# Two value stages of an expert layer: ScalarE's copy, cast and small copy of each block, marked to stand block by block

## The chip, the core and the metric

The kernel runs on one core of one Trainium2 chip. The metric is the device time of one execution in microseconds (us); the time before is the median of three runs, 1945.05 us (1939.61 to 1948.28). The core has five engines that work side by side, each through its own queue in order: TensorE (PE, matrix multiplications into PSUM), VectorE (DVE), ScalarE (ACT), GpSimd (POOL) and SyncE (SP, which here only issues loads). An engine whose next instruction waits for a semaphore stands still, and all that is queued behind that instruction stands with it. Transfers from memory run on 16 DMA engines beside them.

## What is computed

A decoder layer: modulation from a condition vector, a mixing part (sparse attention and retention), and a feed-forward part that picks, for each of 256 tokens and 8 heads, 16 of 16384 experts of one neuron each. The change concerns the end of the feed-forward part:

```
def peer_ffn(h, w_q, sub_keys, w_u, w_v):
    ...
    experts = jnp.take_along_axis(cand_i, pick, axis=-1)
    gates = jax.nn.softmax(top_s, axis=-1)
    ...
    def chunk(args):
        hc, ec, gc = args
        a = jnp.einsum('cd,ced->ce', hc, w_u[ec]).astype(F32)
        coef = (gc * jax.nn.gelu(a)).astype(dt)
        return jnp.einsum('ce,ced->cd', coef, w_v[ec])
```

## The kernel before, in words

For 192 of the tokens the kernel doesn't gather experts: it runs over all 16384 in 128 blocks of 128 experts, first the rows of `w_u` (u stages), then those of `w_v` (value stages), with a coefficient that is zero where a token didn't pick the expert. It does so in two halves of 64 blocks: u stage 1, value stage 1, u stage 2, value stage 2. The other 64 tokens are served by gathers of rows (`gather`, line 800, an indirect DMA on POOL's queue), each followed by one step on DVE over 128x2048 numbers (line 841 or 847). Those steps are spread over the stages by the tables `STEPS`; value stage 1 has 44 of them in its first 58 blocks.

A value stage is the loop of `v_group`. For block j of a stage:

- ScalarE copies the 128x192 coefficients X of the block, rounded to float32r, into a tile `cc` (line 936; here "copy of activations"). There are three buffers of `cc`, so the copy for block j waits until TensorE is through with block j-3.
- DVE subtracts to get the part lost by rounding (line 937), into the same `cc` tile; ScalarE then copies 64 columns of that to their place between the two (line 938; "small copy"). It waits for line 937 of the same block.
- SP loads 1 MB of `w_v` into a `raw` tile (line 147; five buffers). ScalarE rounds it into `whi` (line 156, "cast of the chunk", three buffers), DVE subtracts to get the rest, `wlo` (line 157, two buffers).
- TensorE does 20 multiplications with 512 columns (line 960): 8 that need `whi` and the `cc` tile, 8 that need `wlo`, 4 that need `whi` and the small copy. They add up in eight PSUM banks over all 64 blocks.

The program isn't executed in the order of the source. A scheduler orders the instructions of each engine by its own estimate of time, except those that are marked by `tc.keep_in_program_order` (called `pin` here): among themselves these stay in the order in which they are written. Before, the loads on SP, the gathers on POOL and the steps of lines 841 and 847 on DVE are marked; ScalarE's and DVE's part of a block are not. Lines 156 and 157 lie in the helper `split_to`, and line 147 in `load`.

## Time and profile before

| what | value |
|---|---|
| median of three runs | 1945.05 us |
| the profiled execution: its time, and its span from first to last instruction | 1943.4 us, 1941.6 us |
| busy: TensorE, VectorE, ScalarE, GpSimd | 1826.8, 1479.4, 699.4, 348.6 us |
| mean granted TensorE clock | 0.972 of full speed |
| u stage 1 ends, value stage 1 runs | 1002.6, 1002.6 to 1324.2 us |
| u stage 2 | 1324.2 to 1616.5 us |
| value stage 2 | 1616.5 to 1911.8 us |

The stages before 1002.6 us (the mixing part, the choice of experts and u stage 1) and after are untouched. The engines work at the same time, so their busy times don't add up to the span. Where one of them waits for another counts only if it lies on the chain that ends last.

### The profile page before, as it was taken

To read this page: it belongs to the slowest core of one execution; us is meant where nothing else is said; L and a number is where in the kernel's file an instruction comes from. 1 tells how busy PE (TensorE), PEld (TensorE's weight loads), DVE (VectorE), ACT (ScalarE), POOL (GpSimd) and SP (SyncE) were. 2 spreads that over 40 slices of the span, in tenths; PEclk is the share of its full clock that TensorE was granted. 3 is DMA by queue.
4 is the path that set the end of the run, shared out by engine and by line. 5 is a ranking of instruction groups with operands and counts; after the bars stand their busy time and mean duration, and the time that the engine had idled before them with its cause. 6 is when DMAs were issued, how large, how long until landed. Compare 5 with 4: busy or idle time off the path is not lost.

```text
span 1941.6 us, 28423 instructions
## 1 busy us (share of the span) xinstructions
PE 1826.8 (94%) x11302; PEld 1594.3 (82%) x11302; DVE 1479.4 (76%) x2247; ACT 699.4 (36%) x1192; POOL 348.6 (18%) x254
## 2 busy tenths in 40 slices
PE   5899899999987999989999999999999999999995
PEld 4798778788766899989997767779999998777773
DVE  7877888889985898487578888874455557899875
ACT  3444353635434421021134444451111114555552
POOL 1000001011010012102123323221111212344210
PEclk9999998989988999999999999999999999999998
DMA  8989888989993589989989999989999989999981
GB/s 341 381 310 358 324 303 271 346 287 377 374 321 134 185 297 386 424 319 376 361 357 402 348 382 372 340 307 375 397 357 360 361 303 376 383 394 383 388 323 44
DMA packets 94312, 651.86 MB, mean 336 GB/s; under 512 B 11410, under 2 KB 11586, under 8 KB 18402
## 3 DMA queue, kind: packets, MB, share of 16 engines
q1 hardware_dynamic: 66818, 467.78, 63.6%
q0 software_dynamic: 27360, 182.26, 24.2%
q8 instruction: 89, 1.46, 0.3%
q14 instruction: 45, 0.36, 0.0%
HBM read 643.92 MB, written 4.21 MB: 334 GB/s over the span
## 4 chain that ended last, share of the span: by engine, by line
PE 73%; DVE 11%; DMA 6%; issue 6%; ACT 3%; POOL 0%; SPq 0%; ACTq 0%; POOLq 0%; DVEq 0%
PE acc L960 30%; PE psU L1058 27%; PE psN L449 4%; DVE wlo L157 3%; DMA raw<-in_adaT 2%; DVE raw L197 2%; PE psA L235 2%; PE psD L350 2%; ACT whi L156 2%; PE pg L1043 1%; DMA raw<-in_winA 1%; PE psA L236 1%; PE bkB L350 1%; DMA x2d<-xT 1%; PE bkC L350 1%
## 5 line engine op out<-in xcount | busy, mean ns | idle before, releaser
L157 DVE TENSOR_TENSOR wlo<-raw,whi 128x2048 fp32r<-128x2048 f32 (+2 forms) x215 | 479.3, 2239 | 139.3 <-ACT whi L156 90.0
L1058 PE MATMUL psU<-xT,raw 128*128 128x160 f32 x4096 | 570.8, 301 | 5.8 <-ACT ge L1063 4.5
L1058 PEld LDWEIGHTS psU<-xT,raw 128*128 128x128 f32 x4096 | 560.2, 191 | 6.5 <-ACT ge L1063 4.6
L156 ACT CAST whi<-raw 128x2048 fp32r<-128x2048 f32 (+2 forms) x215 | 400.7, 1869 | 228.0 <-PE psA L235 40.7
L960 PE MATMUL acc<-whi,cc 128*128 128x512 f32 x1512 | 376.3, 396 | 16.7 <-ACT whi L156 16.7
L960 PEld LDWEIGHTS acc<-whi,cc 128*128 128x128 f32 x1512 | 286.6, 190 | 89.4 <-ACT whi L156 19.8
L960 PE MATMUL acc<-wlo,cc 128*128 128x512 f32 x1008 | 257.1, 395 | 2.3 <-DVE wlo L157 2.3
L197 DVE SCALAR_TENSOR_TENSOR raw<-raw,crow 128x2048 f32<-128x2048 f32 x96 | 219.3, 2286 | 21.5 <-DMA raw<-in_adaT 21.4
L960 PEld LDWEIGHTS acc<-wlo,cc 128*128 128x128 f32 x1008 | 164.6, 164 | 66.9 <-DVE wlo L157 5.1
L449 PE MATMUL psN<-whi,act 128*128 128x512 f32 x512 | 166.1, 400 | 2.3 <-ACT sg L628 2.3
L1064 DVE TENSOR_TENSOR X<-X,ge 128x160 f32<-128x160 f32 (+19 forms) x94 | 26.0, 278 | 156.2 <-ACT ge L1063 146.6
L1060 ACT ACTIVATE X<-psU 128x160 f32<-128x160 f32 (+19 forms) x102 | 25.6, 252 | 330.8 <-PE psU L1058 330.7
L449 PEld LDWEIGHTS psN<-whi,act 128*128 128x128 f32 x512 | 95.9, 188 | 25.0 <-ACT sg L628 2.7
L936 ACT CAST cc<-X 128x192 fp32r<-128x192 f32 x128 | 44.8, 353 | 197.1 <-PE acc L960 197.1
L449 PE MATMUL psN<-wlo,act 128*128 128x512 f32 x256 | 103.3, 404 | 3.0 <-DVE wlo L157 2.9
L235 PE MATMUL psA<-act,whi 128*128 128x512 f32 x240 | 87.4, 405 | 8.6 <-ACT whi L156 8.6
L800 POOL DMA_INDIRECT rows<-in_urow,sx x32 | 59.8, 1869 | 130.1 <-DVE rows L841 100.5
L350 PE MATMUL psD<-act,whi 128*128 128x256 f32 x384 | 76.3, 298 | 3.6 <-ACT whi L156 3.6
L800 POOL DMA_INDIRECT xT<-in_v,sx x21 | 57.3, 2727 | 119.6 <-DVE cc L937 76.6
L800 POOL DMA_INDIRECT s<-in_urow,sx x26 | 47.1, 1811 | 145.7 <-DVE s L841 111.6
L841 DVE SCALAR_TENSOR_TENSOR rows<-rows,h2t 128x2048 f32<-128x2048 f32 x32 | 73.0, 2284 | 0.0
L350 PEld LDWEIGHTS psD<-act,whi 128*128 128x128 f32 x384 | 63.2, 201 | 6.4 <-ACT whi L156 4.0
(339 smaller groups left out, 2406.8 us busy)
## 6 DMA issues: line engine op xcount, KB each, us to landing
raw<-in_u SPq DMA_DIRECT2D x128, 1024.0 KB
raw<-in_v SPq DMA_DIRECT2D x128, 1024.0 KB
raw<-in_adaT SPq DMA_DIRECT2D x96, 1024.0 KB
raw<-in_winN SPq DMA_DIRECT2D x16, 1024.0 KB
raw<-in_woutN SPq DMA_DIRECT2D x16, 1024.0 KB
raw<-in_wqT SPq DMA_DIRECT2D x16, 1024.0 KB
raw<-in_winB SPq DMA_DIRECT2D x16, 832.0 KB
raw<-in_winD SPq DMA_DIRECT2D x12, 1024.0 KB
```

The costliest lines, as they stand in the source:

```text
L156: nc.scalar.copy(hi[:, sl], r[:, sl])
L157: nc.vector.tensor_sub(lo[:, sl], r[:, sl], hi[:, sl].bitcast(F32))
L197: nc.vector.scalar_tensor_tensor(r, r, 1.0, crow, op0=OP.mult, op1=OP.mult, accum_out=modc[:, j, k:k + 1])
L235: nc.tensor.matmul(p_, hi[:, sl], act[:, k], start=k == 0, stop=False, skip_group_check=True)
L350: nc.tensor.matmul(bank[:, b, :], x[:, w], y[:, k, :], start=k == k0 and n == 0 and first, stop=k == k1 - 1 and n == 2, skip_group_check=True)
L449: nc.tensor.matmul(ps[tt], x[:, k, ts_], y[:, w], start=k == 0 and j == 0, stop=k == KB - 1 and j == 2)
L800: pin(nc.gpsimd.indirect_dma_start(out=r, out_offset=None, in_=src, in_offset=bass.IndirectOffsetOnAxis(ap=o, axis=0)))
L841: pin(nc.vector.scalar_tensor_tensor(r, r, 1.0, h, op0=OP.mult, op1=OP.mult, accum_out=d[:, e:e + 1]))
L936: nc.scalar.copy(ch, xb(j))
L960: nc.tensor.matmul(acc[c][0:m], x, w[:, c[1] * 512:(c[1] + 1) * 512], start=jj == 0 and n == 0, stop=jj == HALF - 1 and n == 2 - c[0], ski ...
L1058: nc.tensor.matmul(ps, w[:, k * P:(k + 1) * P], xT[:, k, 0:TU], start=k == 0, stop=k == KB - 1)
L1064: nc.vector.tensor_mul(xb(j)[:, 0:done], xb(j)[:, 0:done], ge[:, 0:done])
```

## The change

ScalarE's three instructions of a block are written together: copy of activations, cast of the chunk, small copy. From the fourth block of a stage on (`j > 2`), all three are marked, so that they stand in that order, block after block. The helpers `split` and `split_to` are written out in place, with the same operations on the same tiles; the small copy is written after the cast.

```
-                    nc.scalar.copy(ch, xb(j))
+
+                    inorder = pin if j > 2 else lambda i: i
+                    inorder(nc.scalar.copy(ch, xb(j)))
                     nc.vector.tensor_sub(cl, xb(j), ch.bitcast(F32))
-                    nc.scalar.copy(cc[:, TD:TD + NS], cl[:, P:].bitcast(F32))
-                    chunk = a["v"].rearrange("(e j) d -> j e d", j=P)[hf * HALF + j]
-                    if j <= tail:
-                        hi, lo = split(load(chunk))
-                    else:
-                        hi, lo = pair(j - tail - 1)
-                        split_to(load(chunk), hi, lo)
+                    r = load(a["v"].rearrange("(e j) d -> j e d", j=P)[hf * HALF + j])
+
+                    hi, lo = pair(j - tail - 1) if j > tail else [chunk_tile(n, F32R) for n in ("whi", "wlo")]
+                    inorder(nc.scalar.copy(hi, r))
+                    nc.vector.tensor_sub(lo, r, hi.bitcast(F32))
+                    inorder(nc.scalar.copy(cc[:, TD:TD + NS], cl[:, P:].bitcast(F32)))
```

The old line 936 is line 938 after, 937 is 939, 938 is 945; the casts and subtractions of lines 156 and 157 are lines 943 and 944 after.

What this does to the queues. TensorE, POOL and SP have the same instructions in the same order as before. ScalarE and DVE have the same instructions, some in another order, in both value stages.

ScalarE around block 12 of value stage 1. `cc_8872`, `cc_8905`, `cc_8937`, `cc_8970` are the `cc` tiles of blocks 12 to 15, and `whi_8878`, `whi_8911`, `whi_8943` the casts of blocks 12 to 14 (one number lower in the changed program). Before:

```order
L936 CAST cc_8872<-X0_5979 128x192
L938 CAST cc_8872<-cc_8872 128x64
L936 CAST cc_8905<-X0_5979 128x192
L938 CAST cc_8905<-cc_8905 128x64
L936 CAST cc_8937<-X0_5979 128x192
L156 CAST whi_8878<-raw_8876 128x2048
L938 CAST cc_8937<-cc_8937 128x64
L156 CAST whi_8911<-raw_8909 128x2048
L156 CAST whi_8943<-raw_8941 128x2048
L936 CAST cc_8970<-X0_5979 128x192
```

After:

```order
L938 CAST cc_8872<-X0_5979 128x192
L943 CAST whi_8877<-raw_8875 128x2048
L945 CAST cc_8872<-cc_8872 128x64
L938 CAST cc_8905<-X0_5979 128x192
L943 CAST whi_8910<-raw_8908 128x2048
L945 CAST cc_8905<-cc_8905 128x64
L938 CAST cc_8937<-X0_5979 128x192
L943 CAST whi_8942<-raw_8940 128x2048
L945 CAST cc_8937<-cc_8937 128x64
L938 CAST cc_8970<-X0_5979 128x192
```

Before, the cast of block 12 stands behind the copies of activations of blocks 13 and 14; after, it stands behind that of block 12 alone, and so for every block.

VectorE at the same place; the rows of line 841 are steps on gathered rows, `wlo_8849`, `wlo_8879`, `wlo_8912` the subtractions of blocks 11 to 13 (one lower after). Before:

```order
L157 TENSOR_TENSOR wlo_8849<-raw_8846,whi_8848 128x2048
L937 TENSOR_TENSOR cc_8872<-X0_5979,cc_8872 128x192
L841 SCALAR_TENSOR_TENSOR rows_8627,dots_4922<-rows_8627,h2t_4920 128x2048
L841 SCALAR_TENSOR_TENSOR s2_5985,dots_4922<-s2_5985,h2t_4920 128x2048
L937 TENSOR_TENSOR cc_8905<-X0_5979,cc_8905 128x192
L841 SCALAR_TENSOR_TENSOR rows_8692,dots_4922<-rows_8692,h2t_4920 128x2048
L937 TENSOR_TENSOR cc_8937<-X0_5979,cc_8937 128x192
L157 TENSOR_TENSOR wlo_8879<-raw_8876,whi_8878 128x2048
L157 TENSOR_TENSOR wlo_8912<-raw_8909,whi_8911 128x2048
```

After:

```order
L944 TENSOR_TENSOR wlo_8848<-raw_8845,whi_8847 128x2048
L939 TENSOR_TENSOR cc_8872<-X0_5979,cc_8872 128x192
L841 SCALAR_TENSOR_TENSOR rows_8627,dots_4922<-rows_8627,h2t_4920 128x2048
L841 SCALAR_TENSOR_TENSOR s2_5985,dots_4922<-s2_5985,h2t_4920 128x2048
L841 SCALAR_TENSOR_TENSOR rows_8692,dots_4922<-rows_8692,h2t_4920 128x2048
L944 TENSOR_TENSOR wlo_8878<-raw_8875,whi_8877 128x2048
L939 TENSOR_TENSOR cc_8905<-X0_5979,cc_8905 128x192
L944 TENSOR_TENSOR wlo_8911<-raw_8908,whi_8910 128x2048
L939 TENSOR_TENSOR cc_8937<-X0_5979,cc_8937 128x192
```

The three steps now stand in one piece, the big subtraction of block 12 comes right behind them, and the small subtractions of blocks 13 and 14 come behind the big ones of blocks 12 and 13.

## Rows read from the trace of the kernel before

**Rows 1.** The page: the chain that ended last, by engine.

```profile
PE 73%; DVE 11%; DMA 6%; issue 6%; ACT 3%; POOL 0%; SPq 0%; ACTq 0%; POOLq 0%; DVEq 0%
```

**Rows 2.** Windows, value stages 1 and 2: length, busy us, clock, DMA share, GB/s.

```profile
core 0: us, PE busy (x) PEld busy (x) DVE busy (x) ACT busy (x) POOL busy (x), PEclk, DMA share, GB/s
1002.60:1324.20 321.60, 304.63 (x1283) 232.23 (x1282) 257.60 (x217) 148.41 (x189) 90.84 (x45) 0.97 0.92 357
...
1616.50:1911.80 295.30, 293.19 (x1281) 226.17 (x1281) 247.47 (x165) 147.46 (x185) 96.31 (x39) 1.00 0.91 356
```

**Rows 3.** The chain in value stage 2: start, length, what.

```profile
1624.41 199.59 PE acc L960 x872
```

**Rows 4.** Waits in value stage 1: us in total, times, longest.

```profile
ACT cc L936 <- PE acc L960: 100.7, 60, 3.0
...
PE acc L960 <- ACT whi L156: 16.7, 7, 3.0
...
PE acc L960 <- DVE wlo L157: 0.2, 1, 0.2
```

**Rows 5.** Timeline of ScalarE before block 12: start, length; in brackets the wait.

```profile
1055.53 0.25 ACT L938 CAST cc<-cc 128x64 fp32r<-128x64 f32 x1 [2.21 <-DVE cc L937]
1057.54 0.35 ACT L936 CAST cc<-X 128x192 fp32r<-128x192 f32 x1 [1.76 <-PE acc L960]
1057.80 1.89 ACT L156 CAST whi<-raw 128x2048 fp32r<-128x2048 f32 x1
```

**Rows 6.** Timeline of TensorE around the start of block 12.

```profile
1056.35 1.09 PE L960 MATMUL acc<-whi,cc 128*128 128x512 f32 x4
1059.74 3.38 PE L960 MATMUL acc<-whi,cc 128*128 128x512 f32 x8 [2.30 <-ACT whi L156]
1062.92 2.34 PE L960 MATMUL acc<-wlo,cc 128*128 128x512 f32 x8
1065.10 1.77 PE L960 MATMUL acc<-whi,cc 128*128 128x512 f32 x7
```

**Rows 7.** Windows just behind that wait, same columns as rows 2.

```profile
1059.74:1063.15 3.41, 3.41 (x9) 2.69 (x10) 3.41 (x2) 3.41 (x3) 0.02 (x1) 0.57 1.00 387
```

**Rows 8.** Timeline of VectorE between the big subtractions of blocks 21 and 22.

```profile
1101.50 2.29 DVE L157 TENSOR_TENSOR wlo<-raw,whi 128x2048 fp32r<-128x2048 f32 x1 [1.89 <-issue]
1103.71 2.29 DVE L841 SCALAR_TENSOR_TENSOR rows<-rows,h2t 128x2048 f32<-128x2048 f32 x1
...
1105.92 0.35 DVE L937 TENSOR_TENSOR cc<-X,cc 128x192 fp32r<-128x192 f32 x1
1106.19 2.28 DVE L841 SCALAR_TENSOR_TENSOR s<-s,h2t 128x2048 f32<-128x2048 f32 x1
...
1108.67 2.28 DVE L841 SCALAR_TENSOR_TENSOR rows<-rows,h2t 128x2048 f32<-128x2048 f32 x1
...
1110.89 2.29 DVE L157 TENSOR_TENSOR wlo<-raw,whi 128x2048 fp32r<-128x2048 f32 x1
```

**Rows 9.** Timeline of TensorE there; block 22 begins at 1111.31.

```profile
1110.38 2.90 PE L960 MATMUL acc<-whi,cc 128*128 128x512 f32 x12
1113.24 2.11 PE L960 MATMUL acc<-wlo,cc 128*128 128x512 f32 x8
1115.19 1.54 PE L960 MATMUL acc<-whi,cc 128*128 128x512 f32 x6
```

**Rows 10.** Windows of both value stages, same columns as rows 2.

```profile
1007.00:1057.00 50.00, 50.00 (x220) 38.69 (x219) 42.69 (x36) 22.30 (x31) 13.25 (x7) 1.00 1.00 412
1007.00:1240.00 233.00, 218.99 (x922) 166.67 (x921) 194.94 (x165) 107.63 (x140) 72.43 (x36) 0.97 0.97 378
...
1627.00:1832.00 205.00, 205.00 (x898) 158.49 (x897) 183.88 (x121) 105.63 (x134) 84.19 (x31) 1.00 0.99 392
```

**Rows 11.** DMA issues from 1007 to 1240: count, size, median us to landing.

```profile
raw<-in_v SPq DMA_DIRECT2D x45, 1024.0 KB
s<-in_urow,sx POOLq DMA_INDIRECT x18, 9.7
rows<-in_urow,sx POOLq DMA_INDIRECT x18
```

**Rows 12.** Timeline: a gather's issue and the step that reads it.

```profile
1020.55 2.75 POOL L800 DMA_INDIRECT s<-in_urow,sx  x1 [13.88 <-DVE s L841]
...
1041.59 2.29 DVE L841 SCALAR_TENSOR_TENSOR s<-s,h2t 128x2048 f32<-128x2048 f32 x1
```

**Rows 13.** Waits in value stage 2, as rows 4.

```profile
PE acc L960 <- DVE wlo L157: 2.1, 2, 1.5
```

## Prediction

> **What bounds the kernel now.** I read the chain that ended last first: TensorE holds 73% of it, DMA 6% [rows 1]. What shortens TensorE's idle time inside a stage therefore comes out of the span, as long as nothing else is next in line. Then the two stages that the change touches, side by side [rows 2]. They do the same multiplications, 64 blocks of 20, yet the first takes 321.6 us and the second 295.3 us. TensorE's own pace stands in the chain of the second stage: 872 multiplications in a row in 199.59 us [rows 3], 0.2289 us each. A block of 20 takes 4.58 us, and 1280 of them 293.0 us. So value stage 1 loses 321.6 - 293.0 = 28.6 us, value stage 2 only 2.3 us.

> Where the 28.6 us go is in the waits of stage 1: TensorE waits for ScalarE's cast `whi` 7 times, 16.7 us in all, and for DVE's `wlo` 0.2 us [rows 4]. The timeline at block 12 shows one of the seven. ScalarE stands at the copy of activations of block 14, until TensorE has finished block 11 and so freed a `cc` buffer (1057.54); only then comes the cast of block 12 (1057.80, 1.89 us), which it could have made long before [rows 5]. TensorE, done with block 11 at about 1057.3, needs just that cast and starts at 1059.74 [rows 6]. [...] Seven times: 16.7 + 7 x 1.70 = 28.6 us, which is the whole loss, 4.09 us for each.

> **What the change does to this.** *It removes* the order that makes the seven waits. In the changed order each cast stands right behind the copy of activations of its own block, which waits for TensorE's end of three blocks before. The cast of block 12 is then ready some 0.3 + 0.3 + 1.9 = 2.5 us after the end of block 9 (durations of [rows 5]), and block 12 begins two blocks, 9.2 us, after that end: 6.6 us to spare. This holds for every block, so all seven waits go: -28.6 us.

> *What is late next: `wlo` on VectorE.* At the same places VectorE has three steps of 2.2 us between two big subtractions. Block 22 shows what that costs where ScalarE was in time. The big subtraction of block 21 starts at 1101.50, as soon as TensorE has freed a `wlo` buffer, three steps and two small subtractions follow, and that of block 22 starts at 1110.89 [rows 8]. TensorE's 12 multiplications from 1110.38 then take 2.86 us to the next start instead of 2.75, and the 8 behind them 1.95 instead of 1.83 [rows 9]: 0.23 us lost, no more. The changed order puts one small subtraction less, 0.27 us, ahead of the big one. There are nine such runs in stage 1, two of which (blocks 22 and 37) already pay this. The seven others cost between 0 and 7 x 0.23 = 1.6 us; I take the middle, +0.8. VectorE as a whole has room: 257.6 us busy [rows 2] against 293.

> *What it adds on ScalarE:* the small copy of block 13 now waits for a subtraction that stands behind three steps and the big subtraction of block 12, and behind it are queued the copy and the cast of block 14. On the times of [rows 8], with the 0.27 us less, the big subtraction of block 22 starts at 1110.6, the small one of block 23 at 1112.8, and small copy, copy and cast (0.4 + 0.2 + 0.3 + 1.9) put the cast of block 24 at 1115.6. Block 24 begins at 1111.31 + 2 x 4.58 = 1120.5. TensorE covers this with 4.9 us to spare: 0.

> *Transfers.* No load, gather or issue is moved within its queue, but all of them come closer together, since the buffers come free sooner. From 1007 to 1240 there are 45 loads and 36 gathers of 1024 KB [rows 11], 84.9 MB. Six of the seven waits lie in that window, so the same work would have 233.0 - 6 x 4.09 = 208.5 us: 407 GB/s. Now it gets 378; the first 50 us of the stage, before any wait, ran at 412 with TensorE never idle [rows 10]. By that row it fits and costs 0. But the DMA share there is 1.00, and the other long stretch without waits moved 392 at a share of 0.99 [rows 10]. If 392 were all there is, the window would last 84.9 MB / 392 = 216.6 us, 8.1 us more; if 378, 224.6 us, 16.1 us more. I take 0, since the 412 is from the same stage with the same mix and the 392 is what stage 2 asked for, not shown to be a limit; 0 to 16.1 goes into the range.

> [...]

> *Value stage 2* has the same change, but no wait for a cast; its 2.1 us of waits are two for `wlo` [rows 13], one at its beginning, which the change doesn't reach, and one of 0.6 us around block 47, where a step and a 2048-wide product still stand ahead of the big subtraction. Between -0.6 and +0.6; I take 0. The stages behind are TensorE's too and pass the gain on.

> **The sum,** against the profiled execution: 1943.4 - 28.6 + 0.8 = 1915.6 us. That execution lay 1.65 us under the median of the runs, 1945.05. For the median: 1917 us.

> **Rivals.**
> *Transfers become the bound in part* (chance 0.10). For: 407 GB/s is asked for, at a DMA share that is already 0.97 [rows 10]. Against: the 412 of 50 us. The loads come later by up to five buffers, then casts wait for them. Price 8.1 to 16.1 us: 1925 to 1933.
> *No change* (0.05). Either the transfers are at their limit, or the seven waits turn into waits for another thing at the same places, for instance the clock falling all the same. The order of the queues shows that the change does what it says; that 28.6 us come back in full is against all of rows 8 to 10. 1945.
> *Slower: steps that wait for their gathers* (0.05). VectorE works in order, and nothing is to spare ahead of the big subtraction behind a run of three steps. If the gathers come late there, each of the nine runs holds TensorE up. A gather was issued at 1020.55 and its step started at 1041.59 [rows 12], 21.0 us later, and a landing takes 9.7 us in the median [rows 11]. At the faster pace the 21.0 become 21.0 x 293 / 321.6 = 19.1 us. Landings would have to double before a step waits, and exceed that by 28.6 / 9 = 3.2 us at each run before the change loses. With waits as long as those of today and the slow clock behind them, 9 x 4.09 = 36.8 us: 1945 - 28.6 + 36.8 = 1953 us.

> **Numbers.** The forecast has 0.80, with its own range 1911 to 1922 (0 to 1.6 us at the nine runs, 0.6 us either way in stage 2, and 4 us either way for the runs, which spread from 1939.6 to 1948.3). To hold 8 in 10 with some room I let the range reach into the first rival: 1909 to 1928. About 0.5% (10 us, so below 1935 or above 1955) is what a measurement of this kernel can tell from no change. Forecast and first rival are faster by more: 0.90. No change: 0.05. The slower rival lies around the border, and I count it as slower: 0.05.

> **What would show it.** Right: the list of waits of value stage 1 has no line of TensorE for `whi`; the stage lasts 293 to 295 us with a granted clock of 1.00; GB/s over it near 390. The nine runs right: waits of TensorE for `wlo` of 0.3 us at most. Transfers as the bound: ScalarE's cast waits for `raw`, DMA share 1.00. Wrong altogether: the stage as long as before, with waits of 2 us or more for `wlo`, or VectorE's steps waiting for gathers.

## The result, and the profile after

The changed kernel takes 1917.14 us (median of four runs, 1913.18 to 1919.12); the kernel before, on the same chip, 1944.76 us. The ratio is 0.985, with a 95% interval of 0.983 to 0.988: 27.6 us less. The profiled execution of the changed kernel took 1913.18 us (span 1911.1), against 1943.4 us before.

Three windows of the changed kernel's trace: value stage 1, value stage 2, and the stretch of stage 1 in which the gathers run. The columns are those of [rows 2]: length, busy us of the five engines with their instructions in brackets, granted clock, DMA share, GB/s.

```profile
1002.20:1294.50 292.30, 292.30 (x1281) 226.35 (x1281) 254.94 (x217) 147.90 (x189) 102.21 (x45) 1.00 0.96 393
1586.80:1882.00 295.20, 293.73 (x1284) 226.75 (x1283) 246.41 (x165) 146.77 (x185) 104.44 (x39) 1.00 0.90 356
1007.00:1215.00 208.00, 208.00 (x913) 161.07 (x911) 190.75 (x161) 108.40 (x137) 81.81 (x34) 1.00 1.00 412
```

Value stage 1 has become 29.3 us shorter (321.60 in [rows 2]) and value stage 2 is as long as before (295.30) within a microsecond, so that nearly the whole difference of the two profiled executions, 30.2 us, lies in the one stage. In it TensorE is busy for the whole 292.30 us, at a granted clock of 1.00 instead of 0.97. The chain of waits says the same: in the stage it is one piece, in which TensorE waits for nothing.

```profile
1002.20 292.38 PE acc L961 x1280
```

The list of waits of value stage 1 (us in total, times, longest) has no line of TensorE any more. The line of [rows 4] with 16.7 us for `whi` is gone, and so is the one for `wlo`. These are the first five of the list:

```profile
ACT cc L938 <- PE acc L961: 81.7, 48, 3.2
POOL rows L800 <- DVE rows L841: 69.9, 9, 15.7
ACT cc L945 <- DVE cc L939: 53.1, 26, 4.0
POOL s L800 <- DVE s L841: 47.5, 6, 13.9
DVE wlo L944 <- issue: 31.1, 17, 4.4
```

ScalarE still waits a long time for TensorE at the copy of activations: 81.7 us, against 100.7 in [rows 4]. What has changed is what stands behind that copy. ScalarE's timeline around the same place as [rows 5] (start, length, in brackets the idle time before and who ended it):

```profile
1048.01 0.35 ACT L938 CAST cc<-X 128x192 fp32r<-128x192 f32 x1 [2.26 <-PE acc L961]
1048.27 1.92 ACT L943 CAST whi<-raw 128x2048 fp32r<-128x2048 f32 x1
...
1058.79 0.25 ACT L945 CAST cc<-cc 128x64 fp32r<-128x64 f32 x1 [4.04 <-DVE cc L939]
1058.94 0.35 ACT L938 CAST cc<-X 128x192 fp32r<-128x192 f32 x1
1059.20 1.91 ACT L943 CAST whi<-raw 128x2048 fp32r<-128x2048 f32 x1
```

The first two lines are block 12: copy at 1048.01, cast behind it, done at 1050.2. TensorE begins block 12 at 1056.9, so the cast is 6.7 us ahead, where in [rows 5] it came 2.3 us late. The last three lines are the wait that the change adds: the small copy of block 13 waits 4.04 us for VectorE, which is at its three steps, and the copy and the cast of block 14 stand behind it. That cast is done at 1061.1, and TensorE begins block 14 at 1066.0: 4.9 us ahead.

### The profile page after: what moved, and what is told of

The parts are those of the page before. It is cut to its first block, busy times and chain, and to the rows that moved or that the text cites. A ratio compares the mean times of both kernels' runs of the same rounds, so it can differ in the third digit from the quotient of the medians.

```text
span 1911.1 us, 28440 instructions
## 1 busy us (share of the span) xinstructions
PE 1814.3 (95%) x11302; PEld 1588.9 (83%) x11302; DVE 1476.4 (77%) x2247; ACT 698.0 (37%) x1192; POOL 367.7 (19%) x254
## 4 chain that ended last, share of the span: by engine, by line
PE 75%; DVE 11%; DMA 6%; issue 5%; ACT 2%; POOL 0%; SPq 0%; ACTq 0%; POOLq 0%; DVEq 0%
PE acc L961 31%; PE psU L1059 26%; PE psN L449 4%; DMA raw<-in_adaT 3%; DVE raw L197 3%; DVE wlo L157 2%; PE psA L235 2%; PE psD L350 2%; PE bkB L350 2%; PE pg L1044 1%; PE psA L236 1%; DMA x2d<-xT 1%; PE bkC L350 1%; PE bvB L402 1%; DMA raw<-in_winA 1%
## 5 line engine op out<-in xcount | busy, mean ns | idle before, releaser
L961 PE MATMUL acc<-whi,cc 128*128 128x512 f32 x1512 | 368.1, 391 | 0.0
L944 DVE TENSOR_TENSOR wlo<-raw,whi 128x2048 fp32r<-128x2048 f32 x126 | 288.0, 2286 | 73.4 <-issue 64.0
L961 PE MATMUL acc<-wlo,cc 128*128 128x512 f32 x1008 | 253.0, 391 | 1.5 <-DVE wlo L944 1.5
L156 ACT CAST whi<-raw 128x2048 fp32r<-128x2048 f32 (+2 forms) x89 | 161.1, 1813 | 222.1 <-PE psA L235 41.0
L943 ACT CAST whi<-raw 128x2048 fp32r<-128x2048 f32 x126 | 240.7, 1911 | 0.0
L157 DVE TENSOR_TENSOR wlo<-raw,whi 128x2048 fp32r<-128x2048 f32 (+2 forms) x89 | 192.6, 2168 | 52.7 <-ACT whi L156 36.0
L1061 ACT ACTIVATE X<-psU 128x160 f32<-128x160 f32 (+19 forms) x102 | 25.5, 251 | 334.3 <-PE psU L1059 334.2
L800 POOL DMA_INDIRECT rows<-in_urow,sx x32 | 65.1, 2033 | 108.9 <-DVE rows L841 76.4
L800 POOL DMA_INDIRECT xT<-in_v,sx x21 | 62.7, 2987 | 111.6 <-DVE cc L939 64.9
L800 POOL DMA_INDIRECT s<-in_urow,sx x26 | 53.4, 2053 | 126.2 <-DVE s L841 103.3
```

The lines of the kernel that those rows point to most:

```text
L156: nc.scalar.copy(hi[:, sl], r[:, sl])
L157: nc.vector.tensor_sub(lo[:, sl], r[:, sl], hi[:, sl].bitcast(F32))
L800: pin(nc.gpsimd.indirect_dma_start(out=r, out_offset=None, in_=src, in_offset=bass.IndirectOffsetOnAxis(ap=o, axis=0)))
L943: inorder(nc.scalar.copy(hi, r))
L944: nc.vector.tensor_sub(lo, r, hi.bitcast(F32))
L961: nc.tensor.matmul(acc[c][0:m], x, w[:, c[1] * 512:(c[1] + 1) * 512], start=jj == 0 and n == 0, stop=jj == HALF - 1 and n == 2 - c[0], ski ...
```

## The experiments

Theory A is the prediction's: seven times the cast of a block stood on ScalarE behind the copies of later blocks, whose wait for a buffer held it up; those seven waits and the clock behind them are the gain. The other theories that it is set against are in the expectations. The kernel before, run beside each group of experiments, took 1944.2 to 1945.5 us (medians), so their times can be set against the 1917.14 us of the changed kernel.

### Which stage the gain comes from

```
 e1:  inorder = pin if j > 2 and hf == 0 else lambda i: i
 e2:  inorder = pin if j > 2 and hf == 1 else lambda i: i
```

> The changed order in value stage 1 alone; value stage 2 keeps the order of before. Theory A (the seven waits of TensorE for the cast in stage 1, with the slow clock behind each, are the whole gain): as the changed kernel, 1917 us, stage 1 292 to 293 us without a wait for whi, stage 2 295 us with its 0.6 us at block 47 back. Theory B (part of the gain is the regular spacing of ScalarE's and VectorE's work in both stages): less than the whole gain, between 1917 and 1944 us, some 1930 if both stages share it.

> The changed order in value stage 2 alone; value stage 1 keeps the order of before. Theory A: the seven waits stay, 1944 us (0.6 us at block 47 of stage 2 less, at most). Theory B: some of the gain, below 1940 us.

Measured: stage 1 alone 1917.36 us (ratio 0.985, 0.983 to 0.987), stage 2 alone 1943.78 us (1.000, 0.998 to 1.002). With the order in stage 2 alone, stage 1 has its seven waits back; its list of waits and its window:

```profile
PE acc L961 <- ACT whi L943: 16.7, 7, 3.0
...
1007.10:1328.50 321.40, 304.44 (x1283) 232.26 (x1282) 257.51 (x217) 147.99 (x189) 91.13 (x45) 0.97 0.92 357
```

So the whole gain is stage 1's. The regular order in stage 2 is worth the wait around block 47, if anything: that stage took 294.6 us with it and 295.5 us without. Theory B falls.

### Half of the waits

```
 e3:  inorder = pin if 2 < j < 35 and hf == 0 else lambda i: i
```

> The changed order in blocks 3 to 34 of value stage 1 alone; of the seven waits, those at blocks 12, 17, 27 and 32 are then taken away, those at blocks 42, 47 and 52 stay. Theory A: each wait is worth 4.09 us, so 1917.1 + 3 x 4.09 = 1929.4 us; stage 1 292.4 + 12.3 = 304.7 us, with three waits for whi, 7.2 us in all. Theory C (the time of stage 1 is set by how fast the loads come, and the waits only show where): the loads saved in the first half are waited for in the second, and the gain isn't 4.09 us for each wait; waits of TensorE or ScalarE for raw would show.

Measured: 1927.67 us (ratio 0.990, 0.988 to 0.992), where 1929.4 was expected. The stage's window and its line of TensorE for the cast:

```profile
1009.10:1314.90 305.80, 298.25 (x1283) 229.55 (x1281) 255.79 (x217) 147.75 (x189) 101.49 (x45) 0.98 0.94 376
...
PE acc L961 <- ACT whi L943: 7.6, 3, 3.0
```

Three waits, and 305.8 - 292.3 = 13.5 us more than without any. Nothing that was saved in the first half was waited for in the second. Theory C falls.

The three also give the price of one more exactly than the list of waits does. I took the spacing of the block starts, from the first multiplication of one block to that of the next: 4.57 us where nothing is late. Into a block with a wait it is 2.46 us more (3.13 at block 52), and from that block to the next 1.72 us more, when the clock is down: blocks 41 to 43 of e3 begin at 1196.87, 1203.90 and 1210.19. That is 4.18 us for a usual wait. The list shows only 2.30 of the 2.46. A multiplication is 0.39 us long in the trace and the next starts 0.23 us after it, so a wait that is measured from the end of the last one misses the 0.16 us of overlap.

### The waits put back into the changed kernel

```
+more = 2 if hf == 0 and j % 5 == 2 and 2 < j < 60 else 0
+for k in range(j, j + more + 1):
+    if k not in ccs:
+        ccs[k] = gp_.tile([P, 2 * TD + NS], F32R, name="cc", bufs=3)
+        inorder(nc.scalar.copy(ccs[k][:, 0:TD], xb(k)))
...
```

> The changed kernel, with the order of before put back by hand at every fifth block of value stage 1 from 7 to 57 (eleven places; before had seven waits): ahead of the cast of such a block ScalarE makes the copies of activations of the next two blocks and the small copies of this and the next. Theory A: TensorE waits for the cast at all eleven. By the spacing of block starts in the runs so far a wait costs 2.46 us and the block behind it 1.72 us, 4.18 us together, and 3.09 us at the one in seven where the clock came down later: 11 x 4.18 = 46 us, 1963 us, and 1951 us if all cost 3.09. If the gain of the change were of another origin than these waits (rival): 1917 to 1925 us. VectorE's order at these places is that of before as well.

Measured: 1958.90 us (ratio 1.007, 1.005 to 1.010), 41.8 us over the changed kernel. The stage's waits, its window, and the 3.4 us behind two of its eleven waits, those at blocks 12 and 32:

```profile
PE acc L970 <- ACT whi L949: 25.3, 11, 2.3
...
PE acc L970 <- DVE wlo L950: 0.9, 4, 0.2
...
1007.50:1341.70 334.20, 308.08 (x1284) 232.68 (x1284) 257.77 (x217) 148.05 (x189) 96.03 (x45) 0.96 0.90 344
1067.99:1071.40 3.41, 3.41 (x9) 2.66 (x10) 3.41 (x2) 3.41 (x3) 0.00 (x0) 0.60 1.00 360
1174.97:1178.38 3.41, 3.20 (x13) 2.28 (x14) 3.41 (x2) 3.41 (x3) 0.00 (x0) 1.00 0.96 372
```

All eleven waits are back, and the kernel is slower than before the change; the rival falls. The waits do not all cost the same: seven cost 4.18 us. At the four others (blocks 7, 27, 32, 52) the clock was still at 1.00 in the 3.4 us behind an equal wait of 2.30 us, and the multiplications that use `wlo` then waited 0.2 us for it (the second line). Those cost 3.08 us. The sum, 7 x 4.18 + 4 x 3.08 = 41.6 us, is what the stage lost (334.2 - 292.6 = 41.6 from its first multiplication to its last). The expectation of 46 us counted the full price everywhere.

### The wait and the clock taken apart

```
 e5, on the kernel before (value stage 1):
...
+for h in ([slice(0, 2048)] if hf else [slice(0, 1024), slice(1024, 2048)]):
+    nc.scalar.copy(hi[:, h], r[:, h])
+nc.vector.tensor_sub(lo, r, hi.bitcast(F32))

 e10, on the kernel before:
-hi, lo = split(load(chunk))
+hi, lo = split(load(chunk), parts=1 if hf else 2)
```

> The kernel before, with ScalarE's cast in value stage 1 made in two halves of 1024 columns each, so that TensorE's first multiplications of a block need the first half only. In the built order of ScalarE the cast stands behind the copies of activations of the next two blocks at eight places (blocks 12, 17, 22, 32, 37, 42, 47, 52), so TensorE waits there as before, but for about half as long at once: the copy 0.26 us and a half cast 0.95 us behind TensorE's end of the block before, 1.3 us, and for the second half some 0.5 us more, 1.8 us in all. It tells the two parts of the 4.09 us of one wait apart. If the clock falls only behind the longer waits (theory A, by stage 2 of before, where a wait of 1.47 us left the clock alone): 8 x 1.8 = 14.4 us over the changed kernel, 1931 to 1932 us, granted clock of stage 1 1.00. If the clock falls whatever the length (rival): 8 x (1.8 + 1.7) = 28 us over it, 1945 us, clock 0.97 as before.

> As the run with the cast in halves, and VectorE's big subtraction in halves too, so that its first half needs the first half of the cast only and is no longer late. The built order leaves the cast behind the copies of the next two blocks at nine places; at seven of them (12, 22, 32, 37, 42, 47, 52) the small copy of the last of these stands ahead of the cast too, so that the gap is about 2.1 us, as at block 52 of the run with halves, and 1.44 us at the two others (17 and 27). If the waits alone count: 2 x 1.6 + 7 x 2.3 = 19 us over the changed kernel, 1936 us and clock 1.00. If the clock falls behind the gaps of 2.1 us, as at that block 52: 7 x 1.7 = 12 us more, 1948 us. Stage 2 keeps the order of before or near it.

Measured: 1947.17 us for the first (ratio 1.001, 0.999 to 1.003), 1953.16 us in one run for the second. The first was expected at 1931 or at 1945 us, and neither reason is what happened. TensorE and VectorE at its block 12, and the 3.4 us behind the wait there:

```profile
1068.80 2.13 PE L964 MATMUL acc<-whi,cc 128*128 128x512 f32 x8 [1.44 <-ACT whi L944]
1072.08 2.10 PE L964 MATMUL acc<-wlo,cc 128*128 128x512 f32 x8 [1.14 <-DVE wlo L945]
...
1069.73 6.84 DVE L945 TENSOR_TENSOR wlo<-raw,whi 128x2048 fp32r<-128x2048 f32 x3 [1.54 <-ACT whi L944]
...
1068.80:1072.21 3.41, 2.27 (x9) 1.48 (x10) 2.48 (x2) 3.41 (x5) 0.94 (x1) 1.00 1.00 394
```

TensorE starts earlier, after 1.44 us, and its clock stays at 1.00. But the big subtraction reads both halves of the cast and has not become earlier, so TensorE stands at `wlo` for another 1.14 us. By the spacing of block starts seven such places cost 3.2 us each instead of 4.18; the eighth, block 52, has a gap of 2.11 us, the clock falls behind it (0.61 in the 3.41 us behind the gap), and it costs 4.2. Stage 1 lost 26.8 us in all, 2.5 less than in the kernel before, with eight waits instead of seven, and stage 2 lost 2.4 us more at its first blocks. The price of a wait was thus not the wait and the clock simply added: where the clock did not fall, the next late operand took a part (1.14 us here, 0.2 us in e9).

In the second run VectorE's half is ready in time. Stage 1 lost 33.4 us, close to the 31 that were expected if the clock falls behind the longer gaps. The two places with a gap of 1.44 us there cost 1.8 us each, all told, with the clock at 1.00. At the other seven the gap is 2.1 to 3.1 us; behind six of them the clock fell, at a price of some 1.7 us as in the other kernels, and behind one it did not. Windows behind the waits at blocks 17 (gap 1.44), 37 (2.11) and 32 (3.08):

```profile
1090.70:1094.11 3.41, 3.41 (x15) 2.60 (x16) 3.41 (x4) 3.41 (x5) 0.21 (x1) 1.00 1.03 387
...
1194.76:1198.17 3.41, 3.41 (x9) 2.61 (x10) 3.41 (x4) 3.41 (x4) 0.00 (x0) 0.61 1.00 384
1169.45:1172.86 3.41, 3.41 (x15) 2.61 (x16) 3.41 (x4) 3.41 (x4) 0.50 (x1) 1.00 1.01 420
```

### The small copy ahead of the cast

```
 inorder(nc.scalar.copy(ch, xb(j)))
 nc.vector.tensor_sub(cl, xb(j), ch.bitcast(F32))
+inorder(nc.scalar.copy(cc[:, TD:TD + NS], cl[:, P:].bitcast(F32)))
...
 nc.vector.tensor_sub(lo, r, hi.bitcast(F32))
-inorder(nc.scalar.copy(cc[:, TD:TD + NS], cl[:, P:].bitcast(F32)))
```

> As the changed kernel, but ScalarE's small copy of a block stands ahead of the cast of that block, not behind it (both value stages). The small copy lasts 0.25 us, and the changed kernel's trace shows ScalarE idle for half of the stage. If it is only the place of the casts against the copies of later blocks that counts, this costs nothing: 1917 us. If every wait in front of the cast counts (theory A carried on): the small copy waits for VectorE's small subtraction of its block, which stands behind the big subtraction of the block before and often behind a step of 2.24 us; the big subtraction of the block waits for the cast. Small subtraction, small copy, cast, big subtraction, step then run one behind the other. By the durations of the trace of before (0.33, 0.3, 1.9, 2.24 and 2.24 us) with 35 steps in that loop and 9 beside the cast, 61 blocks take some 6.4 us each instead of 4.57: 105 us more in stage 1, 2022 us, and up to 35 x 1.70 = 60 us beyond that where the clock falls behind the waits; stage 2 as much again at the most. TensorE's waits would be for wlo as well as whi.

Measured: 2090.09 us (ratio 1.074, 1.070 to 1.078), 172.9 us over the changed kernel. Stage 1 takes 86 us more and stage 2 87 us more; the windows of both stages, and the two lines of TensorE in the waits of stage 1:

```profile
1010.24:1388.70 378.46, 315.20 (x1281) 219.17 (x1281) 257.83 (x216) 144.07 (x188) 57.60 (x45) 1.00 0.82 304
1681.20:2063.10 381.90, 316.24 (x1284) 219.28 (x1283) 249.69 (x165) 140.84 (x184) 36.83 (x39) 1.00 0.77 276
...
PE acc L961 <- ACT whi L944: 53.5, 35, 1.5
...
PE acc L961 <- DVE wlo L945: 9.8, 35, 2.4
```

One block of this, from the timeline (VectorE and ScalarE):

```profile
1230.96 0.35 DVE L939 TENSOR_TENSOR cc<-X,cc 128x192 fp32r<-128x192 f32 x1
...
1231.35 0.25 ACT L940 CAST cc<-cc 128x64 fp32r<-128x64 f32 x1 [4.59 <-DVE cc L939]
1231.50 1.90 ACT L944 CAST whi<-raw 128x2048 fp32r<-128x2048 f32 x1
...
1233.42 2.29 DVE L945 TENSOR_TENSOR wlo<-raw,whi 128x2048 fp32r<-128x2048 f32 x1 [2.11 <-ACT whi L944]
...
1235.63 2.28 DVE L841 SCALAR_TENSOR_TENSOR rows<-rows,h2t 128x2048 f32<-128x2048 f32 x1
...
1237.84 0.35 DVE L939 TENSOR_TENSOR cc<-X,cc 128x192 fp32r<-128x192 f32 x1
```

Small subtraction, small copy, cast, big subtraction, step, and the next small subtraction, each waiting for the one before: 6.88 us from 1230.96 to 1237.84 where TensorE needs 4.57. Both engines are idle in turns, and a copy of 0.25 us costs the kernel 173 us by the place where it stands. That the changed order keeps the cast *ahead* of its block's small copy matters as much as that it keeps it ahead of the next copy of activations: no cast waits for VectorE's work on its own block. I had put the loss at 105 us in stage 1 without the clock, from 6.4 us a block. From one small subtraction to the next, 36 rounds of stage 1 took 6.9 us and 22 took 4.7, and the clock never fell (1.00 in both windows).

### Two buffers of activations

```
-cc = gp_.tile([P, 2 * TD + NS], F32R, name="cc", bufs=3)
+cc = gp_.tile([P, 2 * TD + NS], F32R, name="cc", bufs=2)
```

> The changed kernel with two buffers of activations (cc) in place of three, in both value stages. The copy of a block then waits for TensorE's end of two blocks before, not three; by the prediction's working the cast is ready 2.5 us after that end, so 4.57 - 2.5 = 2.1 us to spare instead of 6.6: no wait for whi, 1917 us. VectorE's small subtraction comes one block later too, and with it the steps behind it; in the built order two steps follow each other around a big subtraction once in five blocks, and by the durations of VectorE the big subtraction is then up to 0.3 to 0.6 us late: 12 places, 4 to 7 us, 1921 to 1924 us. If the spare time was worked out wrongly (rival): waits for whi in most blocks, 0.5 us or more in each, 1950 us or more.

Measured: 1924.75 us (ratio 0.990, 0.988 to 0.991), 7.6 us over the changed kernel. No line of TensorE for `whi` is in its waits, so the spare time of the cast was worked out rightly. What costs the 7.6 us is `wlo`, as the second case of the expectation says. The stage's window, and TensorE and VectorE at block 11, one of nine such places (blocks 11 to 51, every fifth):

```profile
1009.60:1310.90 301.30, 295.96 (x1285) 225.51 (x1284) 257.40 (x218) 148.92 (x191) 113.33 (x45) 1.00 0.97 382
...
1062.62 1.65 PE L961 MATMUL acc<-wlo,cc 128*128 128x512 f32 x6 [0.63 <-DVE wlo L944]
...
1060.28 2.28 DVE L944 TENSOR_TENSOR wlo<-raw,whi 128x2048 fp32r<-128x2048 f32 x1
```

Stage 1 is 8.6 us longer, stage 2 1.7 us. The third buffer is thus not needed for the cast; it pays by letting VectorE's small subtractions, and the steps behind them, run earlier, as the expectation has it. (VectorE's built order changed with the number of buffers, so the 8.6 us are not the buffer's alone.)

### What the transfers carry

```
+chunk = a["v"].rearrange("(e j) d -> j e d", j=P)[hf * HALF + j]
+r = load(chunk)
-r = load(a["v"].rearrange("(e j) d -> j e d", j=P)[hf * HALF + j])
+if hf == 0:
+    pin(nc.sync.dma_start(vb.tile([P, 256], F32, name="extra", bufs=4), chunk[:, 0:256]))
 (e8: 512 columns in place of 256)
```

> The changed kernel, and in value stage 1 each block also loads 128 KB of its chunk a second time into a place that nothing reads. It measures what the transfers can carry beyond the 412 GB/s that the changed kernel moved from 1007 to 1215. Asked for in that stretch: (84.9 + 46 x 0.131) MB / 208 us = 437 GB/s. If 412 is the limit (the rival of the prediction stood right behind the edge): 220.7 us instead of 208, 12 us more less the some 5 us by which loads are ahead, so 1924 to 1930 us, with ScalarE's casts waiting for raw and TensorE for the casts. [...]

> As the run before it, with 256 KB more for each block: 466 GB/s asked for. If 412 is the limit: 235.3 us instead of 208, 27 us more less some 5, 1939 to 1944 us. [...] The GB/s over the first 200 us of the stage give the limit itself.

Measured, one run each: 1932.73 and 1945.17 us. Windows of 208 us of stage 1, of the first and the second kernel, and two lines of the first's waits:

```profile
1010.50:1218.50 208.00, 201.22 (x867) 153.69 (x867) 177.93 (x152) 101.47 (x129) 69.30 (x35) 0.99 1.01 414
...
1006.00:1214.00 208.00, 189.97 (x807) 142.08 (x806) 164.78 (x140) 94.33 (x120) 69.30 (x32) 0.99 1.01 412
...
ACT whi L946 <- DMA raw<-in_v: 91.6, 41, 5.5
...
PE acc L964 <- DVE wlo L947: 7.4, 8, 2.1
```

Asked for 437 and 466 GB/s, the transfers carried 414 and 412, and the changed kernel moved 412 without being held up. So over stretches of 208 us some 412 to 414 GB/s is the most that this mix moved in any run, and the changed kernel runs right at it (stretches of 50 us reached more: 421 in the changed kernel, from 1182 to 1232, and 419 in e7, from 1132 to 1182). The price fits: with 128 KB more the stage took 304.6 us, 12 us more than the changed kernel's, as 90.9 MB / 412 = 220.7 us against 208 say; some 1.3 of the 12 us are a fall of the clock behind block 17. I had taken off 5 us for the lead of the loads, which was too much. With 256 KB more the stage is 33.5 us longer. Of these, 4.4 us are no loss: its first multiplication came early, and TensorE went on with those of the stage before. The other 29 are near the 27 worked out. In both the casts wait for `raw`, which they never do in the changed kernel: there each of the 48 loads of the stage whose landing the trace holds landed 2.5 us or more ahead of its cast. The extra loads come in shorter pieces than the others (1 and 2 KB a row instead of 8), so it is not shown that without them the limit would be the same; that the changed kernel has a DMA share of 1.00 at 412 speaks for it.

## Why the prediction was right

The forecast was 1917 us, and 1917.14 was measured. The mechanism was right, as the experiments show; that the two numbers agree to 0.1 us is luck. The sum was made for the profiled execution: it forecast a gain of 27.8 us, and the two profiled executions differ by 30.2. The medians differ by 27.6, and the four runs of either kernel spread over 6 and 9 us. Of the 2.4 us that the sum lacks, 0.2 are in the seven waits, 0.8 and 0.45 at VectorE's runs of steps, and 0.9 in stage 2. Step by step:

- *The seven waits go, 28.6 us.* Right in place and cause: e1, e2, e3 and e9 show that they are the gain, all of it in stage 1, and that each can be taken away or put back by itself. The 1.70 us behind each wait are those of block 12: by [rows 6] the 16 multiplications behind the wait took 5.36 us, where 16 x 0.2289 are 3.66, at a granted clock of 0.57 [rows 7]; by the spacing of block starts it was 1.65 to 1.73 us at six of the seven. Two errors inside this term cancel. Each wait costs 0.16 us more than the list of waits shows (7 x 0.16 = 1.1 us more). And at block 27 the clock did not fall in the 3.4 us behind the wait, so that its second part was 0.62 us and not 1.70 (1.1 us less). By the spacing of block starts the seven cost 28.8 us.
- *6.6 us to spare for the cast.* 6.7 us at block 12. With two buffers (e6) there is still no wait for it.
- *Three steps in a row on VectorE, 0 to 1.6 us, taken as +0.8.* This term was mis-sized: they cost nothing, and the 0.23 us of blocks 22 and 37 went too. Block 22 in the changed kernel, first VectorE's big subtraction, then TensorE:

```profile
1101.90 2.28 DVE L944 TENSOR_TENSOR wlo<-raw,whi 128x2048 fp32r<-128x2048 f32 x1
...
1101.66 2.91 PE L961 MATMUL acc<-whi,cc 128*128 128x512 f32 x12
1104.41 1.77 PE L961 MATMUL acc<-wlo,cc 128*128 128x512 f32 x7
```

  The subtraction starts 0.7 us ahead of its block (1102.59), as the prediction worked out (1110.6 against 1111.31), 0.3 us earlier than in [rows 8]. It ends at 1104.18, and the first multiplication that needs it comes at 1104.41, without a delay. The order took one small subtraction of 0.27 us out of the way, and the delay to be made up was 0.23 us. The prediction had both numbers and took the middle of a range where the difference of the two gave 0. The room is small: at eight of the nine runs (blocks 12 to 47) the subtraction ends 0.22 to 0.23 us ahead of the multiplication that needs it.
- *The small copy behind VectorE's steps, 0, with 4.9 us to spare.* 4.9 us at block 14. e4 shows how much hangs on the small copy standing behind the cast and not ahead of it.
- *Transfers, 0.* Right, but closer than I had said, and in part by luck. The 407 GB/s counted the issues of the window, 84.9 MB. What moved in it was 378 GB/s x 233 us = 88.1 MB [rows 10], which at the faster pace is 422 GB/s, above the 412. Blocks 1 to 46 of the changed kernel, and the rest of the stage:

```profile
1006.60:1216.80 210.20, 210.20 (x922) 162.68 (x921) 192.55 (x163) 108.40 (x137) 83.55 (x35) 1.00 1.00 412
1216.80:1294.60 77.80, 77.80 (x343) 60.33 (x342) 61.42 (x52) 37.45 (x50) 15.21 (x8) 1.00 0.85 338
```

  The first is 86.6 MB: some 1.4 MB came later than before, at the end of the stage, where there was room. The changed kernel never waited for a load. The median from issue to landing, of 1007 to 1215, can be read now:

```profile
raw<-in_v SPq DMA_DIRECT2D x45, 1024.0 KB, 10.1
s<-in_urow,sx POOLq DMA_INDIRECT x17, 10.8
rows<-in_urow,sx POOLq DMA_INDIRECT x17, 12.3
```

  The gathers into `s` took 9.7 us before [rows 11]; for the loads no time of before is known. The rival of the transfers had a chance of 0.10; e7 shows that 128 KB more for each block would have made it true. The 412 GB/s of the first 50 us, [rows 10], which the prediction took for what the transfers can carry, was about the most that they carried over any long stretch. The 392 of stage 2 was no limit for stage 1.
- *Steps that wait for their gathers (the slower rival).* No line of VectorE waiting for a transfer is in the waits of stage 1.
- *Value stage 2, 0 (0.6 either way).* Mis-sized by 0.9 us: from its first multiplication to its last it took 295.5 us before and 294.6 after, as in e2. The wait around block 47 went; by the spacing of block starts it had cost 0.94 us and not 0.6. The 1.5 us at its beginning stayed.

Measured the same way, stage 1 went from 321.9 to 292.6 us. The two stages together make 30.1 of the 30.2 us between the two profiled executions.

## What to carry to other kernels

On an engine that works in order, an instruction that waits for the consumer to free a buffer must not stand ahead of one whose result that consumer needs sooner: here seven such pairs cost 28.8 us. Look for the pair in the timeline as a long wait that ends with the consumer (1.76 us in [rows 5]), followed at once by the instruction the consumer waits for. Price such a wait by the spacing of the consumer's blocks, not by the list of waits alone, and ask what is late next when it goes. When a stage has lost its last gap, compare the GB/s that it will ask for with the most that any stretch of the same mix has moved, and count the bytes that moved, not the issues: here 407 by issues and 422 by bytes stood against 412, and 7 percent more bytes cost 12 of the 29 us again.
